# The low part of the scores' right side in a zero-padded slab for each head

## The chip, the cores and the metric

The kernel runs on one core of a Trainium2 chip. The metric is the device time of one execution in microseconds (us); the lower the better. Several executions are timed and the median is given. The profile is that of one execution.

TensorE multiplies: it loads a stationary matrix (a weight load) and streams the moving one past it, and its results go to PSUM, which has eight banks of 128 partitions x 512 float32 here. ScalarE (ACT), VectorE (DVE) and GpSimd (POOL) do the rest, and SyncE (SP) issues the transfers from the main memory. Each engine takes its own instructions strictly in the order in which the program put them; semaphores make one engine wait for another.

## The reference, cut to what matters

Two layers over 256 tokens of width 1024. Each layer normalizes, makes one input projection, feeds four branches with it (retention, pooling, neighbourhood attention, attention to 256 memory tokens), merges their projections by gates, and ends with a gated feed-forward block:

```python
h = rms_norm(x, norm_mix_g)
rq, rk, rv, rg, pv, nq, nk, nv, mq = jnp.split(h @ w_in, 9, axis=-1)
# retention: scores = q k^T times a decay, no softmax
# neighbourhood and memory attention: softmax(q k^T * d**-0.5 + bias) v, 4 heads x 64
merged = jnp.einsum('bsnd,bsnd->bsd', gates, up)
x = x + merged @ w_out
a, g = jnp.split(rms_norm(x, norm_ffn_g) @ w_ffn_in, 2, axis=-1)
return x + (jax.nn.silu(a) * g) @ w_ffn_out
```

What the change touches is q k^T in three of the branches: four heads of 64 dimensions, 256 x 256 scores a head.

## The kernel before

**Split products.** All is float32. Each operand of a large product is split into a high part that TensorE's fast float32 format holds exactly (hi) and the rest (lo), and a product is made of three: hi hi, hi lo and lo hi. ScalarE casts the high part (whi of a weight, hhi or bhi of an activation), VectorE subtracts to get the low one (wlo, hlo, blo).

**Weights** come in slots of 128 x 1024 (512 KB) in the order of use: four transfer buffers (raw), ten buffers of split halves (NS = 10, whi and wlo). Slots 0 to 3 give q and k of the neighbourhood attention, 4 to 7 its v and the memory's q, 8 to 11 the retention's q and k, 12 to 15 its v and gate, 16 and 17 the pooling values, and gates and the rest follow. The two token tiles t = 0, 1 pass the slots each at its own pace; their sums go to the PSUM banks A0, A1 (t = 0) and A2, A3 (t = 1). A bank is used again for a later block: slots 0 to 3 and slots 8 to 11 both add up in A0 and A2.

**Emptying a bank.** ev_nqk (line 480) empties A0 and A2 after slot 3: it needs the row norm RH, squares the bank (ScalarE), sums by head (VectorE), raises to the power -0.5 (POOL), and scales the bank into w (VectorE). RH itself ends in a power on POOL (rms_chain, line 431). Only then can slot 8 start in that bank.

**Scores.** A score has to multiply hi and lo of both sides as well, but a head has only 64 dimensions, half of the array's 128 rows. to_heads (line 533) therefore puts into LS the high part of a head on its own 64 partitions and the low part on the other 64, and into RS the high part on both; one product of 128 rows then gives hi hi + lo hi. The remaining hi lo is a second product of 64 rows only, on the head's own partitions (line 577):

```python
nc.tensor.matmul(out, LS[:, i, r, tok], RS[:, i, r, :], start=True, stop=False)
nc.tensor.matmul(out, LS[own, i, r, tok], RL[own, r, :], start=False, stop=True)
```

Even heads (i = 0) own the partitions 0 to 63, odd ones 64 to 127. There are 48 such pairs in all: eight products in each of two halves of the two attentions, four for each of the four heads of retention, in two layers.

**The order** is written by the program itself when it is built. Small work is made of chains (generators), and a planner, the class Clock, keeps an estimate of when each engine will be through with what it has been given. A chain goes on when its operands should be there by that estimate; weights are split (pump) when the engines should have caught up; the next slot is given to TensorE when its bank and its weights should be ready. The estimate of an instruction comes from cost (line 80). For POOL it is, whatever the operation, with n the elements of one partition:

```python
if eng == "POOL":
    return 0.3 + 0.17 * n
```

The planner sets the order alone. On the chip an instruction starts when its engine gets to it and its semaphores allow.

Of the kernel before, what the change touches and what calls it, by code (L numbers as in the profile page):

```python
# [9 lines left out]
F32 = mybir.dt.float32  # L10
# [32 lines left out]
class Engine:  # L43
    """An engine of nc whose instructions are also entered in the clock."""

# [18 lines left out]
class Clock:  # L64
    """An estimate in microseconds of when each engine gets to what has been given to it:
    the small work is handed out when its operands should be there, so that no queue waits on it."""

# [80 lines left out]
def tile_encoder(ctx: ExitStack, tc: tile.TileContext, a: dict, out: bass.AP):  # L148
# [5 lines left out]
    def st(shape, dt, name):  # L154
        return sb.tile(shape, dt, tag=name, name=name)
# [21 lines left out]
    RS = st([P, 2, 2, S], F32R, "rs")  # L177
    RL = st([P, 2, S], F32R, "rl")
    SC = [unit(f"sc{i}") for i in range(2)]
# [25 lines left out]

# [1 line left out]
    slots = []  # L207
# [79 lines left out]
    def pump():  # L287
        """split weights when the engines have caught up, the sooner the fewer slots are ready"""
        window = WINDOW[max(0, min(state["lo"] - items[min(pos[0], len(items) - 1)]["j"], len(WINDOW) - 1))]
        if state["urgent"]:  # L290
            window = min(window, 0.8)
        for _ in range(2):
            j = state["lo"]
            if j < state["hi"] and soon(clock.at["DVE"], window) and soon(clock.last(clock.writes, WHI[j % NS])):
                split_lo()
            j = state["hi"]
            if (j < min(n_slots, state["free"] + NS, state["lo"] + NR) and soon(clock.at["ACT"], window)
                    and soon(clock.last(clock.writes, RAW[j % NR]))
                    and soon(max(clock.last(clock.reads, w[j % NS]) for w in (WHI, WLO)))):
                split_hi()  # L300
# [12 lines left out]

# [1 line left out]
    chains = []  # L315
# [16 lines left out]
    def start(gen, *reads):  # L332
        """reads: PSUM banks that gen still reads, until it calls done()"""
        hold(*reads)
        chains.append([clock.now, gen])

    def until(step):
        """a chain goes on after what it has just given out (None), that much later (a number), or at a time"""
        return step[0] if isinstance(step, tuple) else clock.mark + (step or 0)

    def background():
        """let every chain go on whose last instructions should be through"""
        again = True
        while again:
            again = False
            for c in list(chains):
                if soon(c[0], 0.1):
                    clock.mark = clock.now
                    try:
                        c[0] = max(until(next(c[1])), clock.now + 0.15)  # L350
                    except StopIteration:
                        chains.remove(c)
                    again = True
# [28 lines left out]
    def scale_rows(out, in_, col):  # L382
        """out = in_ * col, on the engine that is free sooner"""
        if clock.at["ACT"] < clock.at["DVE"]:
            nc.scalar.activation(out, in_, AF.Copy, scale=col)
        else:
            nc.vector.tensor_scalar_mul(out, in_, col)

# [1 line left out]
    def hi_lo(hi, lo, ps, bank, flag):  # L390
        """hi now, lo when hi is there, which ends the hold on bank"""
        nc.scalar.copy(hi, ps)
        raise_flag(flag + "hi")

        def rest():
            yield from need(flag + "hi")
            nc.vector.tensor_sub(lo, ps, hi.bitcast(F32))
            done(bank)
            raise_flag(flag)

        start(rest())
# [4 lines left out]
    def half_norm(src, t, c, act, gain, flag, bank, pre=None):  # L406
        """Half c of src (token-major) transposed, times gain (there a column), and split.
        What follows the products with it scales by one over the RMS (rms_chain)."""
        urgent = act is act_h
# [21 lines left out]
    def rms_chain(src, rs, junk, flag, after=()):  # L431
        """rs = one over the RMS of each row of src"""
        yield from need(*after)
# [10 lines left out]
    def norm(t, flag, gain, rs, pre):  # L444
        """both halves of the norm of X[t]"""
        for c in range(2):
            start(half_norm(X[t], t, c, act_h, gain, flag, C[c], pre), A[2 * t + c])
        start(rms_chain(X[t], rs, SC[t], flag, halves(flag)))
# [4 lines left out]
    def head_norm(ps, dst, g, scale=None):  # L453
        """dst = ps (times scale, by row) scaled to unit RMS in groups of 64, g of them."""
        ss = sm()
# [16 lines left out]

# [1 line left out]
    def half(u):  # L474
# [56 lines left out]

# [1 line left out]
    def to_heads(left, right, gains):  # L533
        """Token-major [tok, 256], both, to heads with the token in the free dimension, split for scores left^T right:
        LS has hi of a head on its 64 partitions and lo on the others, RS hi on both, and RL lo."""
        yield from acquire(C[0], C[1])
# [30 lines left out]
        for i in range(2):  # L567
            lo(RL[own[i]], C[1], gains[1], i, RS[own[i], i])
        done(C[1])
        yield  # L570

    def scores(out, h, tok):
        """the scores of head h, for the tokens tok of left, with all of right"""
        r, i = h // 2, h % 2
        own = slice(i * HD, (i + 1) * HD)
        nc.tensor.matmul(out, LS[:, i, r, tok], RS[:, i, r, :], start=True, stop=False)
        nc.tensor.matmul(out, LS[own, i, r, tok], RL[own, r, :], start=False, stop=True)

    def attention(l, v, branch, bias):
        """softmax(q k + bias) v for four heads, two at a time, to BHI/BLO[branch]."""  # L580
        yield from acquire(B[0], B[1], C[1])
# [121 lines left out]
    def decay_chain(l):  # L703
        """exp(|i - j| log gamma): the lesser of d lg_fwd and -d lg_bwd, both of which are at most 0 on their side"""
        yield from need(f"memT@{l}", f"dist@{l}", "lg")
# [16 lines left out]
    def prefetch_chain(l):  # L722
        """parameters, and what comes in once the layer's norms are through"""
        nc.sync.dma_start(out=cols, in_=a["cols"][l])
# [32 lines left out]
    def log_sigmoid():  # L757
        """lg = log sigmoid of the 16 decays: min(x, 0) - log1p(exp(-|x|))."""
        t0, t1, t2 = (st([P, 16], F32, f"ls{i}") for i in range(3))
        nc.vector.tensor_scalar_mul(t0, lg, -1.0)  # L760
# [20 lines left out]

# [1 line left out]
    items = []  # L783
    base = [0]

    def add(n_js, act, bank, nk, n=512, first=True, last=True, req=None, end=None, lag=1):
        """bank(t) (+)= act of tile t @ the weights of the next n_js slots; nk k-tiles.
        req: what has to be there; end(t): what follows; lag: slots by which tile 0 may lead here."""
        per = nk // n_js
# [52 lines left out]
    def hid_chain(l, j, t, ps):  # L842
        """silu(a) * g, token-major"""
        yield from need(f"rhf{t}@{l}")
# [24 lines left out]
    def layer(l):  # L869
# [23 lines left out]
        for n, br in enumerate(BRANCHES):  # L893
            for blk in range(2):
                def gate_end(t, blk=blk, bank=on(1 if n == 0 else blk)):
                    start(gate_chain(bank(t), GATE[blk][t], t), bank(t))

                # the gates of the first branch lie around the memory's product
                add(4, act_h, on(1 if n == 0 else blk), KD, lag=5 if n == 3 and blk == 1 else 1, end=gate_end)
# [48 lines left out]
    def ready(t):  # L948
        """when the next slot of tile t can be taken"""
        if pos[t] == len(items) or t == 1 and pos[1] == pos[0]:  # L950
# [33 lines left out]
    def warm(*aps):  # L984
        """products of zeros, which keep TensorE at its full clock until aps are there"""
        while clock.now < max(clock.last(clock.writes, x) for x in aps):
            nc.tensor.matmul(B[0][:, 0:P], W[0][:, 0:P], W[0][:, P:2 * P], start=True, stop=True)
            clock.at["PE"] += 0.21 if clock.now < 6.2 else 0
# [6 lines left out]
    with tc.manual_schedule():  # L995
        nc.vector.memset(W[0][:, 0:P], 0.0)
        nc.vector.memset(mhalf, -0.5)
        def load_x(t, c):
            nc.sync.dma_start(out=X[t][:, HALVES[c]], in_=a["x"][0, t * P:(t + 1) * P, HALVES[c]])
# [45 lines left out]

# [1 line left out]
def _constants():  # L1047
# [69 lines left out]
```

## Time and profile before

| | before |
|---|---|
| time, median of 3 runs (lowest to highest) | 852.66 us (850.24 to 854.39) |
| span of the profiled execution | 850.4 us (its own time is not given beside it) |
| TensorE busy | 840.0 us, 99% |
| weight loads (beside the products) | 678.6 us, 80% |
| VectorE busy | 553.3 us, 65% |
| ScalarE busy | 469.6 us, 55% |
| GpSimd busy | 28.6 us, 3% |
| granted TensorE clock, mean | 0.998 |
| moved by transfers | 152.86 MB, mean 180 GB/s |

Rows of a timeline read: start in us from the span's start, us, engine, line, operation, out<-in by the program's names, partitions x elements of a form, count; in brackets the idle time of the engine before and what ended it. For a product "64*128" means 64 rows by 128 columns of the array. In a product the first name after the arrow streams and the second is the stationary one. Products are pipelined, so that the duration of one (0.39 us) is longer than the step to the start of the next (0.23 us); what counts is the step. All instructions carry line 59, that of the helper which records them. A row by tile has the least, median and greatest duration in ns; a row of a group has busy us and mean ns.

### The profile page before, as it was taken

Reading aid. Unit: us, or ns where it says so; the run is one execution under the profiler, and the core shown is the slowest. Engines: PE = TensorE matmul, PEld = TensorE weight load, DVE = VectorE, ACT = ScalarE, POOL = GpSimd, SP = SyncE. Lnnn points to the kernel's source line nnn. Section 1 sums busy time; section 2 is a strip of 40 time slices with the busy share of each in tenths; the row PEclk is TensorE's granted clock in tenths of the full one; section 3 lists DMA queues with packets and bytes.
Section 4 is the critical chain, followed back from the end, with each engine's and each line's share of the span. In section 5 each row is a group of like instructions: output and inputs, shape, how many; then the busy total and the mean of one; then the engine's idle time right before and its main releaser. Section 6 shows DMA issues by size and latency. Waiting matters only on the chain.

```text
span 850.4 us, 10796 instructions
## 1 busy us (share of the span) xinstructions
PE 840.0 (99%) x3934; PEld 678.6 (80%) x3934; DVE 553.3 (65%) x807; ACT 469.6 (55%) x722; POOL 28.6 (3%) x30
## 2 busy tenths in 40 slices
PE   8999999999999999999999999999999999999998
PEld 7887777778887888888888877777788878888886
DVE  5898776665667656555568778567665775665541
ACT  7867867444556444444469676664454654444430
POOL 0300100000000000000012001000000000000000
PEclk9999999999999999999999999999999999999999
DMA  8946764454558666665363567345554675656611
GB/s 267 315 131 202 246 201 132 131 191 160 191 169 259 188 196 187 186 188 186 96 218 121 173 216 250 134 124 182 165 170 131 190 252 183 190 181 192 193 53 50
DMA packets 103749, 152.86 MB, mean 180 GB/s; under 512 B 6416, under 2 KB 55312, under 8 KB 103696
## 3 DMA queue, kind: packets, MB, share of 16 engines
q1 hardware_dynamic: 103696, 152.17, 56.3%
q8 instruction: 31, 0.51, 0.2%
q14 instruction: 22, 0.18, 0.1%
HBM read 151.10 MB, written 1.05 MB: 179 GB/s over the span
## 4 chain that ended last, share of the span: by engine, by line
PE 94%; DMA 3%; DVE 1%; ACT 1%; SPq 0%; issue 0%; DVEq 0%; ACTq 0%
PE A L59 62%; PE B L59 27%; PE C L59 5%; DMA raw<-in_w_ffn_out 2%; DMA mem<-in_pool_a 1%; DVE wlo L59 1%; DMA x<-in_x 1%; ACT whi L59 1%; DVE w L59 0%; SPq L59 0%; DVE x L59 0%; DVEq L1113 0%; ACTq L59 0%
## 5 line engine op out<-in xcount | busy, mean ns | idle before, releaser
L59 DVE TENSOR_TENSOR wlo<-raw,whi 128x1024 fp32r<-128x1024 f32 (+1 forms) x275 | 329.9, 1211 | 183.6 <-ACT whi L59 182.7
L59 ACT CAST whi<-raw 128x1024 fp32r<-128x1024 f32 x272 | 284.3, 1051 | 221.2 <-PE A L59 102.1
L59 PE MATMUL A<-whi,hhi 128*128 128x512 f32 (+1 forms) x544 | 215.6, 396 | 0.1
L59 PE MATMUL A<-whi,hlo 128*128 128x512 f32 (+1 forms) x544 | 209.4, 385 | 0.0
L59 PE MATMUL A<-wlo,hhi 128*128 128x512 f32 (+1 forms) x544 | 209.0, 384 | 0.0
L59 PEld LDWEIGHTS A<-whi,hhi 128*128 128x128 f32 x544 | 102.4, 188 | 24.1 <-issue 5.5
L59 PEld LDWEIGHTS A<-whi,hlo 128*128 128x128 f32 x544 | 102.4, 188 | 21.2 <-DVE hlo L59 0.5
L59 PEld LDWEIGHTS A<-wlo,hhi 128*128 128x128 f32 x544 | 102.6, 189 | 17.9
L59 PE MATMUL B<-whi,hlo 128*128 128x512 f32 x288 | 112.3, 390 | 0.1
L59 PE MATMUL B<-whi,hhi 128*128 128x512 f32 x288 | 112.3, 390 | 0.0
L59 PE MATMUL B<-wlo,hhi 128*128 128x512 f32 x288 | 112.1, 389 | 0.0
L59 PE MATMUL A<-whi,bhi 128*128 128x512 f32 x272 | 109.2, 401 | 0.0
L59 PE MATMUL A<-whi,blo 128*128 128x512 f32 x272 | 106.3, 391 | 0.0
L59 PE MATMUL A<-wlo,bhi 128*128 128x512 f32 x272 | 106.1, 390 | 0.0
L59 PEld LDWEIGHTS B<-whi,hlo 128*128 128x128 f32 x288 | 54.0, 188 | 12.1 <-DVE hlo L59 0.9
L59 PEld LDWEIGHTS B<-wlo,hhi 128*128 128x128 f32 x288 | 54.1, 188 | 11.2
L59 PEld LDWEIGHTS B<-whi,hhi 128*128 128x128 f32 x288 | 54.1, 188 | 11.1
L59 PEld LDWEIGHTS A<-whi,bhi 128*128 128x128 f32 x272 | 51.1, 188 | 11.4 <-issue 0.8
L59 PEld LDWEIGHTS A<-whi,blo 128*128 128x128 f32 x272 | 51.0, 188 | 11.0
L59 PEld LDWEIGHTS A<-wlo,bhi 128*128 128x128 f32 x272 | 51.2, 188 | 9.7
L59 DVE SCALAR_TENSOR_TENSOR w<-B,rms,w 128x256 f32<-128x256 f32 x72 | 34.6, 482 | 3.9 <-ACT w L59 2.6
L59 ACT CAST bhi<-C 128x512 fp32r<-128x512 f32 x28 | 16.4, 587 | 35.2 <-PE C L59 35.1
(112 smaller groups left out, 614.9 us busy)
## 6 DMA issues: line engine op xcount, KB each, us to landing
raw<-in_w_ffn_in SPq DMA_DIRECT2D x176, 256.0 KB, 3.3
raw<-in_w_gate SPq DMA_DIRECT2D x64, 512.0 KB, 3.8
raw<-in_w_ffn_out SPq DMA_DIRECT2D x44, 512.0 KB, 4.0
raw<-in_w_in SPq DMA_DIRECT2D x36, 512.0 KB, 4.6
raw<-in_w_branch SPq DMA_DIRECT2D x16, 512.0 KB, 5.0
raw<-in_w_out SPq DMA_DIRECT2D x16, 512.0 KB, 4.1
raw<-in_w_mem_kv SPq DMA_DIRECT2D x8, 512.0 KB, 5.1
xn<-in_bias SPq DMA_DIRECT2D x4, 512.0 KB, 5.8
```

What stands on the lines that cost most here:

```text
L59: return f(*args, **kw)
```

## The change

RL, the low part of the right side, gets a slab for each of the two heads of a pair. The slab i holds the head's low part on its own 64 partitions as before, and zeros on the other 64. The second product of a score takes all 128 rows: LS as it stands (high part on its own partitions, low part on the others) against the padded slab, so that lo meets zeros. The zeros are written once, at the program's start, by two memsets on GpSimd of 64 partitions x 512 elements. RL grows from 512 to 1024 elements a partition. The three scratch tiles of the log-sigmoid, 16 elements each, now lie in rgb, which is loaded later. Besides, comments and docstrings are gone.

```diff
@@ -175,7 +175,7 @@
     RS = st([P, 2, 2, S], F32R, "rs")
-    RL = st([P, 2, S], F32R, "rl")
+    RL = st([P, 2, 2, S], F32R, "rl")
...
@@ -565,19 +566,18 @@
         for i in range(2):
-            lo(RL[own[i]], C[1], gains[1], i, RS[own[i], i])
+            lo(RL[own[i], i], C[1], gains[1], i, RS[own[i], i])
         done(C[1])
         yield
 
     def scores(out, h, tok):
-        """the scores of head h, for the tokens tok of left, with all of right"""
+
         r, i = h // 2, h % 2
-        own = slice(i * HD, (i + 1) * HD)
         nc.tensor.matmul(out, LS[:, i, r, tok], RS[:, i, r, :], start=True, stop=False)
-        nc.tensor.matmul(out, LS[own, i, r, tok], RL[own, r, :], start=False, stop=True)
+        nc.tensor.matmul(out, LS[:, i, r, tok], RL[:, i, r, :], start=False, stop=True)
...
@@ -755,8 +755,8 @@
     def log_sigmoid():
-        """lg = log sigmoid of the 16 decays: min(x, 0) - log1p(exp(-|x|))."""
-        t0, t1, t2 = (st([P, 16], F32, f"ls{i}") for i in range(3))
+
+        t0, t1, t2 = (rgb[:, 16 * i:16 * i + 16] for i in range(3))
...
@@ -995,6 +995,8 @@
     with tc.manual_schedule():
         nc.vector.memset(W[0][:, 0:P], 0.0)
         nc.vector.memset(mhalf, -0.5)
+        for i in range(2):
+            nc.gpsimd.memset(RL[(1 - i) * HD:(2 - i) * HD, i].bitcast(F32), 0.0)
```

The memsets enter the planner's clock like any other instruction, so the order of the work changes too, in about the first 570 of TensorE's 3639 rows. Three places show it.

POOL after the change, from its start (sm_139 and sm_140 are the sums of squares of the two token tiles, rms holds the row norms RH):

```order
L1115 UNCONDITIONAL_BRANCH
L59 MEMSET rl_118 64x512 x2
L59 ISA
L59 TENSOR_TENSOR rms_136<-sm1_139,mhalf_137 128x1
L59 TENSOR_TENSOR rms_136<-sm2_140,mhalf_137 128x1
L59 TENSOR_TENSOR rms_136<-sm3_141,mhalf_137 128x1
L59 TENSOR_TENSOR rms_136<-sm4_142,mhalf_137 128x1
L59 TENSOR_TENSOR sm6_144<-sm5_143,mhalf_137 128x8
```

The memsets stand ahead of the powers of the row norms. Behind those of the tokens the two of the memory (sm3, sm4) now come ahead of the first power of ev_nqk (sm5).

VectorE, where A0 is emptied into w0. Before, it comes right behind the split of slot 6 (wlo6), row 19 of the engine:

```order
L59 TENSOR_TENSOR wlo5_88<-raw1_70,whi5_78 128x1024
L59 TENSOR_TENSOR wlo6_89<-raw2_71,whi6_79 128x1024
L59 TENSOR_REDUCE sm3_141<-w0_125 128x8
L59 TENSOR_SCALAR sm3_141<-sm3_141 128x8
L59 TENSOR_SCALAR sm4_142<-sm4_142,rms_136 128x8
L59 TENSOR_TENSOR w0_125<-A0_61,sm4_142 128x512
L59 TENSOR_TENSOR wlo7_90<-raw3_72,whi7_80 128x1024
```

After the change it is row 64:

```order
L59 TENSOR_SCALAR mem1_124<-dist_150,lg_134 128x512
L59 SCALAR_TENSOR_TENSOR mem1_124<-dist_150,lg_134,mem1_124 128x512
L59 TENSOR_REDUCE sm5_143<-w0_125 128x8
L59 TENSOR_SCALAR sm5_143<-sm5_143 128x8
L59 TENSOR_REDUCE sm7_145<-w2_127 128x4
L59 TENSOR_SCALAR sm7_145<-sm7_145 128x4
L59 TENSOR_REDUCE sm9_147<-w1_126 128x8
L59 TENSOR_SCALAR sm9_147<-sm9_147 128x8
L59 TENSOR_REDUCE sm11_149<-w2_127 128x4
L59 TENSOR_SCALAR sm11_149<-sm11_149 128x4
L59 TENSOR_SCALAR sm6_144<-sm6_144,rms_136 128x8
L59 TENSOR_TENSOR w0_125<-A0_61,sm6_144 128x512
```

In between stand now, in this order: the splits of slots 7 to 17 with the low parts of the memory's norm (blo) among them, the log-sigmoid, and the four decay tables (dist, lg and mem). ScalarE has the matching high parts, exponentials and, only behind them, the square of A0.

TensorE at the first product of slot 8 (whi8 into A0). Before:

```order
L59 MATMUL A3_64<-whi6_79,hlo1_96 128x512
L59 MATMUL C0_67<-ident_gain_131,mem0_123 128x128 x4
L59 MATMUL A3_64<-whi6_79,hhi1_94 128x512
L59 MATMUL A3_64<-wlo6_89,hhi1_94 128x512
L59 MATMUL A3_64<-whi6_79,hlo1_96 128x512
L59 MATMUL A3_64<-whi7_80,hhi1_94 128x512
L59 MATMUL A3_64<-wlo7_90,hhi1_94 128x512
L59 MATMUL A3_64<-whi7_80,hlo1_96 128x512
L59 MATMUL A3_64<-whi7_80,hhi1_94 128x512
L59 MATMUL A3_64<-wlo7_90,hhi1_94 128x512
L59 MATMUL A3_64<-whi7_80,hlo1_96 128x512
L59 MATMUL A0_61<-whi8_81,hhi0_93 128x512
```

After the change:

```order
L59 MATMUL A3_64<-whi7_80,hhi1_94 128x512
L59 MATMUL A3_64<-wlo7_90,hhi1_94 128x512
L59 MATMUL A3_64<-whi7_80,hlo1_96 128x512
L59 MATMUL C0_67<-ident_gain_131,mem0_123 128x128 x4
L59 MATMUL C0_67<-ident_gain_131,mem1_124 128x128 x8
L59 MATMUL A0_61<-whi8_81,hhi0_93 128x512
```

The three further groups of memory transposes, each of which needs the bank C0 emptied by ScalarE and VectorE first, have come ahead of slot 8; they stood behind it before. SP's order changes in one place: the load of rgb comes ahead of slot 22's, where it came some 14 slots later.

## The prediction

> **What bounds the kernel now.** I read the page's totals first, then the waits of TensorE, then the timelines around the scores, then the first 70 us engine by engine.
>
> ```profile
> span 850.4 us, 10796 instructions
> PE 840.0 (99%) x3934; PEld 678.6 (80%) x3934; DVE 553.3 (65%) x807; ACT 469.6 (55%) x722; POOL 28.6 (3%) x30
> ...
> PE C L59 <- DVE w L59: 2.8, 4, 1.1
> PE C L59 <- DMA x<-in_x: 2.4, 1, 2.4
> PE B L59 <- DVE mhalf L59: 1.1, 1, 1.1
> ```
>
> TensorE is busy for 840.0 of 850.4 us, and all its waits that the trace names come to 6.3 us. So a microsecond taken from TensorE's stream is a microsecond of the kernel, and a microsecond in which TensorE has nothing to do is lost for good, since almost no slack is left in which to make it up. Both happen here, at two different places.
>
> **Term 1: the scores get shorter.** The timeline of one block of scores, eight products, and of one block of four in retention:
>
> ```profile
> 45.80 0.28 PE L59 MATMUL B<-rs,ls 128*128 128x256 f32 x1
> 46.01 0.38 PE L59 MATMUL B<-rl,ls 64*128 64x256 f32 x1
> 46.32 0.38 PE L59 MATMUL B<-rs,ls 128*128 128x256 f32 x1
> ...
> 48.20 0.66 PE L59 MATMUL C<-ident_gain,mem 128*128 128x128 f32 x4
> ...
> 145.23 0.28 PE L59 MATMUL B<-rs,ls 128*128 128x256 f32 x1
> ...
> 146.38 0.50 PE L59 MATMUL A<-whi,bhi 128*128 128x512 f32 x1
> ```
>
> From start to start two neighbours are 0.31 us apart, although they stream only 256 columns. The nearest row with 256 columns and 128 rows throughout is the pooling projection, which also loads weights before every product (the page counts as many loads as products, 3934):
>
> ```profile
> 61.77 0.28 PE L59 MATMUL A<-whi,hlo 128*128 128x256 f32 x1
> 61.89 0.28 PE L59 MATMUL A<-whi,hhi 128*128 128x256 f32 x1
> ...
> 64.29 0.28 PE L59 MATMUL A<-whi,hlo 128*128 128x256 f32 x1
> ```
>
> There the starts are 0.12 us apart (2.52 us for the 21 steps from 61.77 to 64.29). What differs is that the scores change between 128*128 and 64*128 at each product. After the change all 96 are 128*128, so I price each at 0.12. A block of eight falls from 48.20 - 45.80 = 2.40 to 0.96, by 1.44; a block of four from 146.38 - 145.23 = 1.15 to 0.48, by 0.67. Two attentions with two blocks each and four retention blocks, in two layers, make eight of each: 8 x 1.44 + 8 x 0.67 = 16.9 us. Bounds: if the first product of a block (0.21 us from 45.80 to 46.01) is the price of all, 8 x 0.72 + 8 x 0.31 = 8.2 us; above, 18 us if the slow first product behind a block (0.50 at 146.38) goes too. I take 16.9, since the 0.12 rows have the very shape. That twice the rows are multiplied costs nothing: time goes by columns in both rows.
>
> **Term 2: TensorE runs dry near the start.** The two added memsets are on POOL, and the planner that writes the order charges a POOL instruction 0.3 + 0.17 us per element of a partition: 87.3 us for 512 elements, 174.7 for both. Behind them on POOL stands the power that gives the row norms. So the planner believes that no norm is there before 175 us, and hands out all else first: the split of ten more slots, the whole memory norm, the log-sigmoid and the decay tables. On chip nothing waits for 175 us, but the queues are in order. The squares and the scaling that empty A0 now stand behind that work, and slot 8's product, which overwrites A0, behind them. POOL itself:
>
> ```profile
> L59 POOL TENSOR_TENSOR sm<-sm,mhalf 128x8 f32<-128x8 f32 x6 | 10.8, 1795 | 154.3 <-DVE sm L59 154.3
> L59 POOL TENSOR_TENSOR rms<-sm,mhalf 128x1 f32<-128x1 f32 x12 | 6.6, 554 | 366.8 <-DVE sm L59 366.8
> L1106 POOL MEMSET const-float32-0.0<- 128x1 f32 x1 | 0.1, 98 | 0.2 <-issue 0.2
> ...
> 16.74 0.55 POOL L59 TENSOR_TENSOR rms<-sm,mhalf 128x1 f32<-128x1 f32 x1 [16.30 <-DVE sm L59]
> ```
>
> A memset of one element takes 0.1 us; a power grows by (1795 - 554) / 7 = 177 ns per element. A memset of 64x512 is nearer the first, and POOL idles until 16.74: up to 8 us each, both are hidden. I take nothing for them.
>
> When does TensorE run dry, and when does it go on? Before:
>
> ```profile
> 30.98 0.60 PE L59 MATMUL C<-ident_gain,mem 128*128 128x128 f32 x4
> 31.34 0.48 PE L59 MATMUL A<-whi,hhi 128*128 128x512 f32 x1
> ...
> 33.51 0.39 PE L59 MATMUL A<-whi,hhi 128*128 128x512 f32 x1
> ...
> 25.91 0.69 DVE L59 TENSOR_TENSOR w<-A,sm 128x512 f32<-128x512 f32 x1
> ...
> 30.91 1.23 DVE L59 TENSOR_TENSOR wlo<-raw,whi 128x1024 fp32r<-128x1024 f32 x1
> ```
>
> Nine products after the memory's first transposes (31.34), slot 8 starts at 33.51; A0 had been emptied at 25.91. The order up to there is the same work in both kernels, so TensorE will have nothing left at about 33.5 but three groups of memory transposes, 0.36 each (30.98 to 31.34), which come earlier than before: 1.1 us of its work. VectorE is at the same place in both kernels when it splits slot 10 (30.91 to 32.05). Behind that it has, in order, up to the emptying of A0:
>
> ```profile
> 28.44 3.69 DVE L59 TENSOR_TENSOR wlo<-raw,whi 128x1024 fp32r<-128x1024 f32 x3
> 32.05 0.21 DVE L59 TENSOR_SCALAR cols<-cols 128x1 f32<-128x1 f32 x2
> ...
> 34.03 1.13 DVE L59 SCALAR_TENSOR_TENSOR blo<-C,ident_gain,bhi 128x128 fp32r<-128x128 f32 x4
> ...
> 62.77 0.39 DVE L59 SCALAR_TENSOR_TENSOR ls<-ls,ls 128x16 f32<-128x16 f32 x2
> ...
> L59 DVE SCALAR_TENSOR_TENSOR mem<-dist,lg,mem x8: 742/749/752, 76.2 to 473.0; 128x512 f32<-128x512 f32 x8
> L59 DVE TENSOR_SCALAR mem<-dist,lg x4: 479/482/484, 78.0 to 459.9; 128x512 f32<-128x512 f32 x4
> ...
> 22.92 0.68 DVE L59 TENSOR_REDUCE sm<-w 128x8 f32<-128x512 f32 x1
> ...
> 23.89 1.65 POOL L59 TENSOR_TENSOR sm<-sm,mhalf 128x8 f32<-128x8 f32 x1 [4.28 <-DVE sm L59]
> ...
> 25.57 0.23 DVE L59 TENSOR_SCALAR sm<-sm,rms 128x8 f32<-128x8 f32 x1 [1.76 <-POOL sm L59]
> ```
>
> Seven splits (slots 11 to 17) at 1.2 (28.44 to 32.05 is three): 8.4. Four groups of blo at 1.05: 4.2. Six small ones: 0.8. Some seventeen dependent log-sigmoid steps at 0.195: 3.3. Decay tables, 4 x 0.75 + 3 x 0.48: 4.4. Reduction with its scalar step 0.8, power 1.7, scaling 0.3 + 0.7. Sum 24.6, and 32.05 + 24.6 = 56.7: that is when A0 is empty if VectorE never waits.
>
> It will wait, on ScalarE above all:
>
> ```profile
> 31.49 0.63 ACT L59 ACTIVATE qk<-mem 128x512 f32<-128x512 f32 x1
> ...
> 32.88 1.12 ACT L59 ACTIVATE bhi<-C,ident_gain 128x128 fp32r<-128x128 f32 x4
> ...
> 29.82 1.05 ACT L59 CAST whi<-raw 128x1024 fp32r<-128x1024 f32 x1 [0.30 <-DMA raw<-in_w_in]
> ...
> 80.30 0.63 ACT L59 ACTIVATE mem<-mem 128x512 f32<-128x512 f32 x1
> ...
> raw<-in_w_in SPq DMA_DIRECT2D x18, 512.0 KB, 5.9
> ```
>
> Laid beside each other by these rows (the two squares of a memory tile take 1.4, 31.49 to 32.88; four bhi 1.1; a cast 1.0), VectorE loses about 1.4 us at the memory's squares and the first high parts, 1.2 at later high parts and at slot 17's transfer (issued when slot 13 is split, some 5 us to land), 1.2 at the log-sigmoid's exponential and the first scaled table, which ScalarE does, and 1.7 at the end, where the last exponential (0.63), a copy and the square of A0 stand between the last table and the reduction: 5.5 us. So A0 is empty, and slot 8 starts, at about 62. Bounds: 56.7 without any wait; 68 if the waits are twice that. The loss is 62 - 33.5 - 1.1 = 27.4 us (22.1 to 33.4). All later main products queue behind this one; nobody catches it up, since TensorE had no slack.
>
> The stop is also felt in the clock. The table by stretches, for the first 11.4 us, in which TensorE starts and pauses (behind the five engines' busy times stands the granted clock):
>
> ```profile
> 0.00:11.40 11.40, 7.91 (x38) 7.21 (x38) 3.88 (x13) 5.75 (x12) 0.20 (x4) 0.85 0.81 270
> ```
>
> The granted clock was 0.85, that is 0.15 x 11.4 = 1.7 us lost. No row shows the clock after a stop in the middle of the program, so the bounds are 0 and twice that, 3.4; since some 20 us pass without a product, longer than any pause at the start, I take 1.7. The Trainium skill, "TensorE: Matmul & The Clock Gate", section "What's actually happening", has the clock fall to half after an idle window and come back after some 3.4 us of work; an estimate by it is 1.7 us, where a clock that never falls in mid-program would leave the sum at 860.9.
>
> Costed at nothing: the RL slab has the same writers, sizes and readers but for the zeros; the log-sigmoid's scratch in rgb delays only rgb's load, which on SP stands ahead of slot 22's load, and that waits for a later split anyway (if not, one landing, 5.9 us, mostly behind ten split slots); from about row 570 of TensorE on, the order is the old one. At the first scores the low part comes within about 1 us of its reader; 0 to 2 us, taken as 0.
>
> **Sum:** 850.4 + 27.4 + 1.7 - 16.9 = 862.6 against the span, +12.2. The median of the runs shown, 852.66, is 2.3 above that span (the profiled execution's own time is not given), so the forecast is 852.7 + 12.2 = 864.9, slower by 1.4%.
>
> **Rivals.** *Not slower: the backlog drains faster.* Place: VectorE between slot 10's split and A0. Every microsecond that slot 8 starts earlier than 62 is one less; at 54 the kernel is within 0.5%. That needs VectorE to run without any wait and its own sum to be 2.7 us smaller than by the rows; at 53 the time is 855.9. For it: steps that don't depend on each other start before the last one ends (the two at 62.77 take 0.39 together, and the step at 32.05 starts 0.08 before the splits from 28.44 end). Against: the chain to A0 crosses ScalarE and POOL several times. 12%.
>
> *The scores gain nothing.* If a weight load cannot run under a product of the same rows, each score pays load and product in turn, which is the 0.31 of now: 852.7 + 29.1 = 881.8. Against: the 0.12 rows have such loads. 5%. This is what the Trainium skill, "TensorE: Matmul & The Clock Gate", section "The mechanism", states (overlap only where the row groups differ); the trace disagrees with it at 61.77.
>
> *The memsets cost what the planner thinks.* At 177 ns per element, 181 us for both; the norms and A0 come at about 190, and the time is 852.7 + (190 - 34.6) + 1.7 - 16.9 = 993. 3%.
>
> **Numbers.** The forecast holds 80%. Runs of this kernel can tell about 0.5% from no change (848.4 to 856.9). Of the 12%, 3 lie below that band and 9 in it, with 3 of the forecast's own low end: faster 3%, same 12%, slower 85%. The range from the bounds: low 22.1 + 0 - 18 is +4, 857; high 33.4 + 3.4 - 8.2 is +29, which I cut to 874, since all three would have to go wrong together.
>
> **What would show it.** Right: scores at 0.12 from start to start, all 128*128; a hole of about 28 us in TensorE's row from 33.5, broken by three short transposes, released by w<-A on VectorE at 62; a granted clock well below 1 for some 3 us behind it; the rest of the kernel unchanged. Wrong: a hole that ends before 54, scores at 0.2 or more, POOL's memsets beyond 8 us, or new holes behind the first.

## The result

| | before | after |
|---|---|---|
| time, median of 4 runs each (lowest to highest) | 852.4 us (850.24 to 854.39) | 862.99 us (861.97 to 863.87) |
| ratio to before, with its 95% interval | | 1.0137 (1.0119 to 1.0154) |
| span of the profiled execution | 850.4 us | 862.1 us (its own time 863.87, 1.8 more, the longest of its four) |

The kernel became slower by 1.4%, through two effects of opposite sign. The page of after, its totals, and of the 40 slices the rows of TensorE and its granted clock:

```profile
span 862.1 us, 10816 instructions
PE 825.5 (96%) x3934; PEld 675.3 (78%) x3934; DVE 554.6 (64%) x805; ACT 469.7 (54%) x722; POOL 27.7 (3%) x32
...
PE   8619999999999999999999999999999999999998
...
PEclk9859999999999999999999999999999999999999
```

TensorE's busy time fell by 14.5 us (840.0 to 825.5), and yet the span grew by 11.7. The second and third slice, from 21.6 to 64.7 us, show why: TensorE is busy for 6 and 1 tenths there, and its clock is low. The waits of TensorE name the cause:

```profile
PE A L59 <- DVE w L59: 20.3, 1, 20.3
PE C L59 <- DVE blo L59: 6.6, 3, 2.8
```

One wait of 20.3 us and three of together 6.6 are new. TensorE's timeline there:

```profile
32.08 0.40 PE L59 MATMUL A<-whi,hlo 128*128 128x512 f32 x1
33.87 0.66 PE L59 MATMUL C<-ident_gain,mem 128*128 128x128 f32 x4 [1.39 <-DVE blo L59]
37.31 1.11 PE L59 MATMUL C<-ident_gain,mem 128*128 128x128 f32 x4 [2.78 <-DVE blo L59]
40.81 1.12 PE L59 MATMUL C<-ident_gain,mem 128*128 128x128 f32 x4 [2.40 <-DVE blo L59]
62.27 0.77 PE L59 MATMUL A<-whi,hhi 128*128 128x512 f32 x1 [20.34 <-DVE w L59]
62.83 0.63 PE L59 MATMUL A<-wlo,hhi 128*128 128x512 f32 x1
...
67.10 0.61 PE L59 MATMUL A<-whi,hlo 128*128 128x512 f32 x1
67.52 1.06 PE L59 MATMUL C<-ident_gain,w 128*128 128x128 f32 x8
```

After slot 7 (its last product at 32.08) there is nothing but three groups of transposes until slot 8 at 62.27, where A0 is empty at last. Behind it twelve products take from 62.27 to 67.52, 0.43 us each instead of 0.23. The table by stretches has the granted clock (the last but two of the numbers in a row):

```profile
0.00:11.40 11.40, 8.70 (x45) 7.58 (x46) 4.50 (x14) 6.75 (x16) 1.24 (x6) 1.00 0.83 265
45.00:58.00 13.00, 0.00 (x0) 0.00 (x0) 10.01 (x28) 4.97 (x9) 0.00 (x0) 0.50 0.52 173
62.00:66.00 4.00, 3.73 (x9) 2.99 (x10) 2.35 (x7) 0.00 (x0) 2.69 (x3) 0.50 0.00 0
70.00:80.00 10.00, 9.68 (x47) 7.95 (x46) 8.52 (x12) 6.95 (x11) 0.00 (x0) 1.00 0.32 104
```

And the gain: a block of eight scores after the change, the row of all second products by tile, and, from the kernel before, the second product behind a block of four.

```profile
90.55 0.28 PE L59 MATMUL B<-rs,ls 128*128 128x256 f32 x1
90.66 0.27 PE L59 MATMUL B<-rl,ls 128*128 128x256 f32 x1
...
91.48 0.40 PE L59 MATMUL A<-whi,hhi 128*128 128x512 f32 x1
...
L59 PE MATMUL B<-rl,ls x48: 274/283/356, 73.3 to 588.2; 128*128 128x256 f32 x48
...
146.71 0.40 PE L59 MATMUL A<-wlo,bhi 128*128 128x512 f32 x1
```

The block takes 0.93 us (91.48 less 90.55), from 2.40, and from the product behind it to the next are 0.23 us, where before there were 0.33 (146.71 less 146.38).

One landmark separates the two. The last small products of the pooling branch stand behind all scores of their layer, in both kernels. In the timelines of before they start at

```profile
180.53 1.08 PE L59 MATMUL B<-w,cols 64*64 64x256 f32 x8
...
599.70 1.08 PE L59 MATMUL B<-w,cols 64*64 64x256 f32 x8
```

and in those of after at

```profile
201.55 1.08 PE L59 MATMUL B<-w,cols 64*64 64x256 f32 x8
...
611.32 1.08 PE L59 MATMUL B<-w,cols 64*64 64x256 f32 x8
```

From one to the other it is 419.2 us before and 409.8 after: the second layer's scores alone give 9.4 us, so both layers, taken as equal, 18.8. At the first landmark the kernel is 21.0 us late, with one layer's gain already in it; at the end it is 11.7 late.

### The profile page after: what moved, and what is told of

Its sections match the earlier page's. It is cut to its first block, busy times and chain, and to the rows that moved or that the text cites. A ratio compares the mean times of both kernels' runs of the same rounds, so it can differ in the third digit from the quotient of the medians.

```text
span 862.1 us, 10816 instructions
## 1 busy us (share of the span) xinstructions
PE 825.5 (96%) x3934; PEld 675.3 (78%) x3934; DVE 554.6 (64%) x805; ACT 469.7 (54%) x722; POOL 27.7 (3%) x32
## 4 chain that ended last, share of the span: by engine, by line
PE 86%; DMA 5%; DVE 4%; ACT 3%; issue 1%; POOL 1%; SPq 0%; DVEq 0%; ACTq 0%; POOLq 0%
PE A L59 56%; PE B L59 25%; PE C L59 4%; DMA raw<-in_w_in 2%; DVE wlo L59 2%; DMA raw<-in_w_ffn_out 1%; ACT whi L59 1%; DMA mem<-in_pool_a 1%; DMA x<-in_x 1%; POOL sm L59 1%; DVE sm L59 1%; DVE mem L59 0%; DVE w L59 0%; DVE hlo L59 0%; ACT qk L59 0%
## 5 line engine op out<-in xcount | busy, mean ns | idle before, releaser
L59 PE MATMUL A<-whi,hhi 128*128 128x512 f32 (+1 forms) x544 | 215.7, 397 | 20.4 <-DVE w L59 20.3
L59 PEld LDWEIGHTS A<-wlo,hhi 128*128 128x128 f32 x544 | 103.1, 189 | 18.1 <-DVE wlo L59 0.2
```

The source lines that it names most:

```text
L59: return f(*args, **kw)
```

## The experiments

Each run also timed the kernel before on the same chip; times are medians, ratios are to that one.

**The memsets without their charge.** The padded slab and its memsets stay, but the memsets are given to the engine past the planner, so that it knows nothing of them:

```diff
-            nc.gpsimd.memset(RL[(1 - i) * HD:(2 - i) * HD, i].bitcast(F32), 0.0)
+            tc.nc.gpsimd.memset(RL[(1 - i) * HD:(2 - i) * HD, i].bitcast(F32), 0.0)
```

> The padded slab with its two memsets on POOL, but the memsets are not entered in the planner's clock, so that TensorE's order is that of the kernel before. Theory (two separate terms, -18.8 us from the scores and +30.5 us from the hole at the start): no hole, slot 8 at about 33, blocks of eight scores in 0.95 us, time 852.4 - 18.8 = 833.6 us (831 to 836). Rival (part of the gain seen in the changed kernel came from the ten slots split ahead, not from the scores): 838 to 845 us. Rival (the memsets on POOL themselves delay the row norms): a hole stays, over 845 us.

Measured: 833.87 us against 851.99, ratio 0.979 (0.977 to 0.982), 18.1 us faster. TensorE's waits and the memsets in this kernel:

```profile
PE C L59 <- DVE w L59: 2.5, 4, 0.8
...
L999 POOL MEMSET rl<- x2: 518/518/519, 0.7 to 1.3; 64x512 f32 x2
```

The four waits for w come to 2.5 us together, and no single wait of TensorE is longer than 1.1: there is no hole. TensorE's instructions stand in the trace in exactly the order of the kernel before. The memsets are the same instructions on the same engine, 0.52 us each, over by 2 us. So neither they nor the padded products cost anything; what cost was the planner's belief about them. The gain is that of the scores alone, and the ten slots split ahead had no part in it.

**The charge without the padding.** The changed kernel, but the second product takes its 64 rows again:

```diff
-        nc.tensor.matmul(out, LS[:, i, r, tok], RL[:, i, r, :], start=False, stop=True)
+        own = slice(i * HD, (i + 1) * HD)
+        nc.tensor.matmul(out, LS[own, i, r, tok], RL[own, i, r, :], start=False, stop=True)
```

> The changed kernel, memsets and order as they are, but the second product of a score takes 64 rows again. Theory: the hole alone, 852.4 + 28.9 (hole) + 2.4 (clock) - 1.2 (the earlier start of that one execution, which is chance) to + 0.5 = 881 to 884 us; blocks of eight scores back at 2.40 us. Rival (the terms are not separate: with slow scores TensorE hides part of the hole): 870 to 878 us.

Measured: 882.47 us, ratio 1.036 (1.034 to 1.039), 30.5 us slower. The wait and a score of it:

```profile
63.84 0.77 PE L59 MATMUL A<-whi,hhi 128*128 128x512 f32 x1 [20.27 <-DVE w L59]
...
75.00 0.38 PE L59 MATMUL B<-rs,ls 128*128 128x256 f32 x1
75.32 0.38 PE L59 MATMUL B<-rl,ls 64*128 64x256 f32 x1
```

The hole is there at full length without the padding, and the rival's 870 to 878 us is out. -18.1 and +30.5 make +12.4; the changed kernel itself is at +10.6 (862.99 - 852.4), and at +11.9 when it was run again (864.68 - 852.78, below). The two effects simply add, within the spread of the medians.

**A smaller charge.** The changed kernel, with a memset on POOL charged at 15.6 us instead of 87.3:

```diff
+        if eng == "POOL" and op == "memset":
+            return 0.3 + 0.03 * n
         if eng == "POOL":
             return 0.3 + 0.17 * n
```

> The changed kernel, but the planner charges a memset on POOL 0.3 + 0.03 us per element, 15.6 us each and 31.2 for both, instead of 87.3 each. The emptying of A0 now stands behind the split of slot 12 on VectorE, at row 40 instead of 64. Theory (the hole is as long as the work that stands ahead of A0 in VectorE's and ScalarE's queues): slot 8 starts at 43 to 44 us, the hole is some 11 us with the transposes in it, time 833.6 + 10 + 1.5 (clock) = 845 us (842 to 849). Rival (the hole follows the planner's charge in proportion, 31 of 175): 833.6 + 0.18 x 29 = 839 us. Rival (any charged memset breaks the start in the same way): 863 us.

Measured: 843.77 us, ratio 0.992 (0.989 to 0.994), in the range of the theory; both rivals, 839 and 863, are out.

```profile
33.23 0.66 PE L59 MATMUL C<-ident_gain,mem 128*128 128x128 f32 x4 [1.26 <-DVE blo L59]
36.66 1.11 PE L59 MATMUL C<-ident_gain,mem 128*128 128x128 f32 x4 [2.78 <-DVE blo L59]
40.94 1.11 PE L59 MATMUL C<-ident_gain,mem 128*128 128x128 f32 x4 [3.16 <-DVE blo L59]
42.42 0.77 PE L59 MATMUL A<-whi,hhi 128*128 128x512 f32 x1 [0.36 <-DVE sm L59]
```

Slot 8 starts at 42.42 instead of 62.27, a little earlier than the 43 to 44 expected. The first two gaps are those of the changed kernel; what is gone is the stretch in which the log-sigmoid, the decay tables and five splits stood ahead of A0. The hole is as long as the queue ahead of A0, and the charge acts only through the order that it leads to. (With half the full charge, 43.8 us a memset, the planner writes the same order on all engines as with the full one; no run shows its time.)

**The clock behind the hole.** The changed kernel with 80 products ahead of slot 8 that nobody reads, not known to the planner; the changed kernel again beside it.

```diff
+        if pos[t] == 8 and t == 0:
+            for _ in range(80):
+                tc.nc.tensor.matmul(B[0], HHI[0][:, 0, :], WHI[j % NS][:, 0:512], start=True, stop=True)
```

> The changed kernel with 80 products of 512 columns that nobody reads, put into TensorE's queue ahead of slot 8, where it would stand idle from 42 to 62; they are not entered in the planner's clock, and the rest of the order is the same. They end at about 42 + 8 x 0.43 + 72 x 0.23 = 62 us. Theory (behind the hole the clock is at half, 12 products at 0.43 instead of 0.23 and some transposes): slot 8's products start 0.23 apart, time 863.0 - 2.4 = 860.6 us, a ratio to the kernel before some 0.003 lower than the changed kernel's. Rival (the wide steps behind the hole come from something else, such as weights that are read for the first time): no change, 863 us.

> The changed kernel once more, on the chip of the three beside it, as their yardstick: 863 us, 1.3% above the kernel before (1.011 to 1.015).

Measured: 861.45 us, ratio 1.0095 (1.0076 to 1.0114); the changed kernel 864.68, ratio 1.0136 (1.0110 to 1.0161). The difference of 0.004 has the size and sign expected, but the intervals overlap slightly, so the times do not decide. The timeline is plain:

```profile
41.60 20.48 PE L967 MATMUL B<-whi,hhi 128*128 128x512 f32 x80
...
63.27 0.47 PE L59 MATMUL A<-whi,hhi 128*128 128x512 f32 x1 [1.19 <-DVE w L59]
63.58 0.40 PE L59 MATMUL A<-wlo,hhi 128*128 128x512 f32 x1
```

Behind the first, the products of slot 8 start 0.23 us apart at once, and the granted clock from 62 to 66 us is 1.00 instead of 0.50. The operands are the same as in the changed kernel, and wlo and hlo, which the extra products do not read, step by 0.23 as well. So the 0.43 of the changed kernel was the clock, which stays up here where TensorE was kept busy. The Trainium skill, "TensorE: Matmul & The Clock Gate", section "What's actually happening", has half clock after an idle window of 3.4 us; the 0.50 in the table above agrees.

**Memsets on VectorE.** The changed kernel with `nc.vector.memset` in place of `nc.gpsimd.memset`, entered in the planner's clock like all else.

> The changed kernel with its two memsets on VectorE, where the planner charges 0.07 + 0.00055 us per element, 0.35 us each. Theory (only the charge for POOL broke the start): TensorE's order is that of the kernel before and the time that of the uncharged memsets, 833.9 us (832 to 836). Rival (VectorE is needed at the start, and the memsets put off the first low parts): 835 to 837 us.

Measured: 835.1 us, ratio 0.979 (0.976 to 0.981), the same as the uncharged memsets within their intervals. By itself the time fits the theory's range and the rival's, which meet at 835 to 836. The trace decides for the theory: TensorE's order is that of the kernel before, and the two memsets are over at 2.3 us on a VectorE that is idle from there until 6.1. This and the first experiment are both faster than either kernel, by 2.1%.

**What in 64 rows is slow.** The kernel before, without padding, with the products of a block regrouped: all of 128 rows first, then all of 64.

```diff
+        for out, h, tok in parts:
...
+            nc.tensor.matmul(out, LS[:, i, r, tok], RS[:, i, r, :], start=True, stop=False, ...)
+        for out, h, tok in parts:
...
+            nc.tensor.matmul(out, LS[own, i, r, tok], RL[own, r, :], start=False, stop=True, ...)
```

Two sums that share a PSUM bank are begun here before either is finished, and the scores do not come out whole; all products are run, and only their time counts.

> The kernel before, with the scores of a block regrouped: first all products of 128 rows, then all of 64 rows, nothing padded. Theory (what costs is the change between 64 and 128 rows, about 0.19 us each): two changes in a block instead of eight or four, a block of eight in 0.96 + 2 x 0.19 = 1.34 us, a block of four in 0.86 us, time 852.4 - 8 x 1.06 - 8 x 0.29 = 841.6 us (839 to 845). Rival (a 64-row product is slow by itself, whatever stands beside it): blocks stay at 2.40 us, 852 us.

Measured: 838.28 us, ratio 0.984 (0.981 to 0.987), 13.7 us faster where 10.8 were expected.

```profile
43.95 0.63 PE L59 MATMUL B<-rs,ls 128*128 128x256 f32 x4
44.52 0.51 PE L59 MATMUL B<-rl,ls 64*128 64x256 f32 x4
44.95 0.66 PE L59 MATMUL C<-ident_gain,mem 128*128 128x128 f32 x4
...
146.10 0.40 PE L59 MATMUL B<-rs,ls 128*128 128x256 f32 x2
146.43 0.50 PE L59 MATMUL B<-rl,ls 64*128 64x256 f32 x2
146.85 0.50 PE L59 MATMUL A<-whi,bhi 128*128 128x512 f32 x1
147.19 0.40 PE L59 MATMUL A<-wlo,bhi 128*128 128x512 f32 x1
```

The rival falls: a 64-row product is not slow by itself. Eight products take 1.00 us instead of 2.40 with two changes of the row count, four take 0.75 instead of 1.15. The 0.19 for each change comes out, one way as the other, but it lies on both sides of the change. In the block of four the steps from start to start are 0.11, 0.21, 0.22 and 0.21, and the product behind takes 0.34 (147.19 less 146.85) instead of 0.23: each change adds some 0.09 to the product ahead of it and some 0.10 to the one behind. With 0.12 for a product, two changes make 0.48 + 0.38 = 0.86, of which 0.10 falls behind the block. The same count gives the blocks of before: 0.96 + 8 x 0.19 - 0.10 = 2.38. What goes beyond the count is the block of eight here: its four 64-row products (two heads, both halves of the partitions) take hardly longer than two, 0.43 against 0.42.

**The same in pairs over two banks**, so that a bank never has more than one unfinished sum: two of 128 rows, two of 64 rows on different halves, twice a block; retention as before.

> The kernel before, unpadded, with the attention scores regrouped by pairs of banks: two products of 128 rows, then two of 64 rows (one on each half of the partitions), twice a block. Retention's blocks stay as before. Theory (a fixed cost for each change of the row count): from the grouped kernel's blocks of four, 0.75 us for two and two, a block of eight takes 1.5 us against 2.40, time 852 - 8 x 0.9 = 844.8 us; if the two 64-row products on different halves run at the same time, 1.26 us and 842.9 us. Rival (a 64-row product costs 0.31 us by itself): 852 us.

Measured: 843.45 us, ratio 0.989 (0.987 to 0.991).

```profile
68.51 0.39 PE L59 MATMUL B<-rs,ls 128*128 128x256 f32 x2
68.83 0.38 PE L59 MATMUL B<-rl,ls 64*128 64x256 f32 x2
69.14 0.50 PE L59 MATMUL B<-rs,ls 128*128 128x256 f32 x2
69.57 0.38 PE L59 MATMUL B<-rl,ls 64*128 64x256 f32 x2
69.89 0.50 PE L59 MATMUL A<-whi,hhi 128*128 128x512 f32 x1
```

A block takes 1.38 us, between the 1.5 and the 1.26 expected. The two 64-row products take 0.31 together (68.83 to 69.14), what one took before: on different halves they run at the same time. With four changes at 0.19 and two products hidden the count is 0.96 + 0.76 - 0.24 - 0.10 = 1.38. So regrouping gives half of the gain (9.3 of 18.1 us) without a slab; padding gives all of it.

## Why the prediction was right

The forecast was 865 (+12.2 us on the span); the span grew by 11.7, the median by 10.6. Term by term:

| term | predicted | measured | from |
|---|---|---|---|
| scores | -16.9 (-18 to -8.2) | -18.8; alone -18.1 | landmarks; first experiment |
| hole ahead of slot 8 | +27.4 (22.1 to 33.4) | +28.9 | 62.27 less 32.3 less 1.1 |
| clock behind it | +1.7 (0 to 3.4) | +2.5 | 12 products, 67.52 - 62.27 against 12 x 0.23 |
| first scores late | 0 (0 to 2) | +0.6 | first block 1.53 us (73.23 to 74.76) less 0.95, behind a wait for rl |
| start of the program | not a term | -1.2 | memory's transposes at 29.79, before at 30.98 |

The measured terms make +12.0, within 0.3 of the span. The mechanism was right in both parts. That the sum lies so near is partly luck: the terms are off by -1.9, +1.5, +0.8, +0.6 and -1.2, which nearly cancel.

The last term belongs to neither kernel. TensorE's wait for the first x is 2.4 us in the profile of before and 1.4 in that of after, and over all the profiles this wait and the clock of the first 11.4 us go together: 0.4 to 1.5 us and a clock of 1.00 in seven, 2.4 to 2.7 us and 0.85 to 0.87 in three (before, the kernel with 80 products, the memsets on VectorE). Padded and unpadded kernels are in both groups, so the change has no part in it.

*The scores.* The blocks came out as priced, 0.93 to 0.95 for 0.96 and 0.47 for 0.48. What was left out of the value, the slow product behind each block (0.10 us, sixteen times), is most of the missing 1.9; it stood in the upper bound of 18, which the 18.8 still passes a little. The regrouped kernels show that the choice of the row was right for the right reason: the change between 64 and 128 rows was the cost, not the columns or the rows. The rival in which they gain nothing is gone, and with it, for these products, the rule of the Trainium skill, "TensorE: Matmul & The Clock Gate", section "The mechanism", that a load runs under a product only where their row groups differ: here loads and products of the same 128 rows follow each other every 0.12 us while a load takes 0.19.

The rows of the weight loads show what a change of the row count does. The first row is from before, the second from after:

```profile
46.32 0.19 PEld L59 LDWEIGHTS B<-rs,ls 128*128 128x128 f32 x1
...
90.55 0.19 PEld L59 LDWEIGHTS B<-rl,ls 128*128 128x128 f32 x1
```

Among equal rows the load starts a step ahead of its product (90.55 for the product at 90.66), under the one before. In the alternating block it starts only with its own product (both at 46.32). A load of 0.19 that is no longer covered, and 0.12 for the product, are the 0.31 of a step. So what the rival says of every load holds where the row count changes. That the uncovered load is the whole of the 0.19 fits these rows; no run tests it by itself.

*The hole.* VectorE's own timeline, with the waits that were added up beforehand:

```profile
32.69 1.12 DVE L59 SCALAR_TENSOR_TENSOR blo<-C,ident_gain,bhi 128x128 fp32r<-128x128 f32 x4 [0.63 <-ACT bhi L59]
34.99 1.23 DVE L59 TENSOR_TENSOR wlo<-raw,whi 128x1024 fp32r<-128x1024 f32 x1 [0.53 <-ACT whi L59]
39.63 1.13 DVE L59 SCALAR_TENSOR_TENSOR blo<-C,ident_gain,bhi 128x128 fp32r<-128x128 f32 x4 [1.25 <-ACT bhi L59]
46.92 1.22 DVE L59 TENSOR_TENSOR wlo<-raw,whi 128x1024 fp32r<-128x1024 f32 x1 [0.38 <-ACT whi L59]
52.57 0.75 DVE L59 SCALAR_TENSOR_TENSOR mem<-dist,lg,mem 128x512 f32<-128x512 f32 x1 [0.58 <-ACT mem L59]
58.51 0.69 DVE L59 TENSOR_REDUCE sm<-w 128x8 f32<-128x512 f32 x1 [1.64 <-ACT w L59]
61.43 0.69 DVE L59 TENSOR_TENSOR w<-A,sm 128x512 f32<-128x512 f32 x1
```

With two more of 0.24 and 0.28 the waits are 5.5 us, as predicted, and A0 is empty at 62.1 against 62 predicted. (VectorE is some 0.5 us earlier here at the end of slot 10's split, 31.5 for 32.05, and its own work up to A0 some 0.5 longer than added up; that the moment fits to 0.1 is chance.) The loss is 1.5 larger than predicted, 0.3 of it at this end and 1.2 at the other: this execution began earlier, and TensorE ran dry at 32.3 instead of 33.5, which the last row of the table gives back. In the second run of the changed kernel and in the one with the charge alone the same reckoning gives 28.6 and 28.0. The rival of a faster backlog is out: restart was to come before 54, and came at 62.27. So is that of memsets at the planner's price: 0.52 us each.

*The clock.* The size was near, but its row was a poor witness, so the 1.7 is in part luck. The 0.85 of the first 11.4 us in the profile of before is not a property of the kernel: in the profile of after the same stretch has 1.00. What carried the term is that the clock is 0.50 in the hole and for 3 to 5 us behind it, which no row of before could show. How long it stays low differs from one execution to the next. Behind the same hole 12 products ran at half clock in the profile of after, 10 in that of the charge alone, and 7 in that of the changed kernel run again; from slot 8's first product to the transposes behind its twelve the loss is 2.5, 2.2 and 1.5 us.

*The sign.* It came from putting the planner's charge for the two memsets (174.7 us for 1.04 us of work) beside the order that it leads to. Without that, the change is a gain of 2.1%.

## What to carry to other kernels

Where a model in the program sets the order, a new instruction is first of all a new entry in that model: look up what it is charged before you look at what it costs, for a wrong charge is paid by the engines behind it, through the order, and many times over. Products that alternate between 64 and 128 rows pay for each change; padding with zeros takes that away, and grouping equal shapes a part of it. And at a TensorE that is busy for 99%, price both signs and add them: here -18 and +30 were each larger than what was left.

## What the runs showed of the hardware that was not expected

- A change of the row count, from 128 to 64 or back, costs about 0.19 us with products of 256 columns, some 0.09 on the product ahead and 0.10 on the one behind. A pair takes 0.63 us in alternation and 0.23 at equal rows.
- Two 64-row products on different halves of the partitions run at the same time (0.31 us for both); two on the same half take 0.42.
- The clock takes a varying time to come back. Behind the hole of 20 us it was 7, 10 and 12 products at half clock (3.1, 4.4 and 5.2 us) in three executions, and behind the shorter hole of the smaller charge 8 products, 3.6 us.
- A memset of 64 x 512 float32 takes 0.52 us on GpSimd and 0.49 on VectorE (1.1 for two on either), where a power of 128 x 8 on GpSimd takes 1.6.
